# A streaming encoder step on one core: the last feed-forward down projection done with plain products, and the first pair of down weights begun one up tile sooner

## The chip, the cores and the metric

The kernel runs on one core of a Trainium2 chip. The time is that of one execution on the device, in microseconds (us); the kernel before was timed three times, at 1915.1, 1917.89 and 1915.02 us, with a median of 1915.1 us. One more execution was profiled.

## The reference, cut to what matters

The reference is one step of a two-layer encoder in float32, with a model width of 1024 and 544 tokens (512 of a prompt and 32 of a running stream). Layer 0 mixes tokens with a state-space block, layer 1 with retention; each layer then has a cross-attention to a memory and a convolutional feed-forward block (FFN), and one normalisation ends the step. The change concerns the FFN:

```python
def conv_ffn(h, conv_state, w_up, conv_w, conv_b, w_down):
    u = h @ w_up                       # 1024 -> 2 x 2816
    a, g = jnp.split(u, 2, axis=-1)
    ext = jnp.concatenate([conv_state, a], axis=1)
    conv = cw[0] * ext[:, 0:l] + cw[1] * ext[:, 1:l + 1] + cw[2] * ext[:, 2:l + 2] + conv_b
    y = (jax.nn.gelu(conv) * g) @ w_down   # 2816 -> 1024
# every layer:  x = x + conv_ffn(rms_norm(x, norm_ffn[i]), ...)
```

## The kernel before: tiles, stages and order

All activations are kept transposed, 128 features on the partitions by 544 tokens. So x is eight tiles `x[0..7]` of 128x544, and the 2816 hidden features are 22 tiles. Tokens are worked in two halves of 272 (`TH`), since a product of one half fills one bank of the accumulator.

Each float32 product is made of three passes of a reduced type: an operand is split into a high part (`hi`, a cast on ScalarE, L228) and a low part (`lo = value - hi`, on VectorE, L229), and hi.hi, hi.lo and lo.hi are added up on TensorE (PE). A plain projection (`dense`, with `dense_k`, L269) takes for each tile of 128 outputs 6 matmuls of 128x272 per tile of 128 inputs (two halves by three passes): 48 with the eight tiles of x. `dense2` does the first two outputs of a projection together, all but the last `late` input tiles first (by default one), so that they can begin before the last input tile is ready.

The FFN goes through its 22 hidden tiles in groups of 8, 8 and 6 (`FGROUPS`). For each tile it makes the two up products ("an up tile": 96 matmuls), the convolution, the gelu and the product with the gate (`gr`). After each group, `down` adds this group's share of the down projection to x. It does so by a Strassen-Winograd scheme with seven products in place of eight: the group's tiles are paired (`kps` pairs: 4, 4, 3), the eight output tiles are paired (p = 0..3), and each pair takes seven products, `step(p, 1)` to `step(p, 7)`, each of 3 x kps matmuls on one half (L1240). So a group of eight takes 4 x 7 x 12 = 336 matmuls, where a plain projection would take 384, and the group of six takes 252, where a plain one would take 288. Each product is added to x from the accumulator by VectorE (`add`, L1244, 128x272). Products that share an accumulator tile wait for each other's add.

The seven products need sums of weights. `unit` makes them for half an output pair's weights (a unit has at most two of the kps pairs, and pairs 0..3 have two units each): a load of the raw blocks on SyncE's queue (L1153, buffer `wr`), the sums `ws` on VectorE and GpSimd (L1163 to L1165; one buffer), the high part `hb` of the three plain blocks a11, a22, a12 (ScalarE, L1166), `lb = -hb` (ScalarE, L1167), the high part `wh` of the sums (ScalarE, L1174), a DMA from GpSimd's queue that reads the three blocks from memory again and adds them into `lb` (L1177, accumulate), and the low part `wl` of the sums (VectorE, L1180). `tokens` makes the matching sums of the hidden tiles (L1200 to L1203).

`begin` loads and starts the first unit of pair 0, `more` its DMA and the second unit; `rest` does all else: calls of `step` in a fixed order, with `load`, `make` and `close` of the next pair's units between them. Both are called around the up products of the group's last tile. The buffers are shared with the plain projections: `wr`, `wh` and `wl` have three slots each (one extra `wh` and `wl` for each fourth unit), `hb` and `lb` four, the accumulator four tiles `ps`. A scheduler orders each engine's instructions from the program's order and its own estimates; each engine then runs its list strictly in order.

When a tile of x is final after the last group, `resid_done` prepares what comes next. In layer 0 this is retention: the split of x times a gain (ScalarE L327 `xh`, VectorE L328 `xl`), the square (L334) and its sum `acc` (GpSimd, L337); the sum over features is made on PE (L365, L376) inside retention's first `dense2`, which has `late=2`. In layer 1 it is the end of the kernel: square, sum, y = x times a gain (L341), transposes of y on PE (L439), the sums of squares on PE (L365), scaling (L444, L445) and the stores. `add_x` (L392) is the add of a plain projection, 128x544.

Of the kernel before, what the change touches and what calls it, by code (L numbers as in the profile page):

```python
# [9 lines left out]
F32 = mybir.dt.float32  # L10
# [7 lines left out]
P = 128  # L18
# [81 lines left out]
def w_pairs(w):  # L100

    a = w.reshape(w.shape[0] // P, P, KT // 2, 2, P)
    out, kp = [], 0
    for nk in unit_sizes(a.shape[0] // 2):
        for mi, ki in ((1, 0), (0, 0), (1, 1), (0, 1)):
            out += [a[2 * (kp + n) + ki, :, :, mi].transpose(1, 0, 2) for n in range(nk)]
        kp += nk
    return np.concatenate(out, axis=2)


def layout(inp):
# [53 lines left out]
    d["w_g"] = np.stack([w_tiles(f["ffn_w_up"][i][:, FF:]) for i in range(2)])  # L165
    o = 0
    for n, g in enumerate(FGROUPS):
        d[f"w_d{n}"] = np.stack([w_pairs(f["ffn_w_down"][i][o * P:(o + g) * P]) for i in range(2)])
        o += g
    d["conv"] = np.concatenate([cols(a) for i in range(2) for a in (f["ffn_conv_w"][i], f["ffn_conv_b"][i][None])], axis=1)  # L170
    d["cconv"] = f["cache_conv"][:, 0].reshape(2, 2, NF, P).transpose(3, 0, 2, 1).reshape(P, 2 * NF * 2)
# [21 lines left out]
class Kernel:  # L193
# [945 lines left out]
    def unit(self, src, nk, j):  # L1139


        V, A, PL = self.nc.vector, self.nc.scalar, self.nc.gpsimd
        n = nk * P
        d, t = {}, {}

        def buf(tag):
            if j % 4 == 1:
                return self.fp.tile([P, 1024], F32R, tag=tag + "x", bufs=1, name=self.name(tag))
            return self.main.tile([P, 1024], F32R, tag=tag, bufs=3, name=self.name(tag))

        def load():
            t["raw"] = self.main.tile([P, 1024], F32, tag="wr", bufs=3, name=self.name("wr"))
            self.nc.sync.dma_start(out=t["raw"][:, :4 * n], in_=src)  # L1153

        def sums():
            raw = t["raw"]
            t["hs"], t["ls"] = buf("wh"), buf("wl")
            t["hb"], t["lb"] = (self.fp.tile([P, 768], F32R, tag=g, bufs=4, name=self.name(g)) for g in ("hb", "lb"))
            sf = t["sf"] = self.fp.tile([P, 1024], F32, tag="ws", bufs=1, name=self.name("ws"))[:, :4 * n]

            def two(a):
                return a.rearrange("p (b n) -> p b n", b=2)
            V.tensor_tensor(out=two(sf[:, :2 * n]), in0=two(raw[:, n:3 * n]), in1=raw[:, :n].unsqueeze(1).to_broadcast([P, 2, n]), op=OP.subtract)  # L1163
            V.tensor_tensor(out=sf[:, 2 * n:3 * n], in0=sf[:, n:2 * n], in1=raw[:, n:2 * n], op=OP.add)
            PL.tensor_tensor(out=sf[:, 3 * n:], in0=raw[:, 3 * n:4 * n], in1=sf[:, 2 * n:3 * n], op=OP.subtract)  # L1165
            A.copy(t["hb"][:, :3 * n], raw[:, n:4 * n])  # L1166
            A.activation(out=t["lb"][:, :3 * n], in_=t["hb"][:, :3 * n].bitcast(F32), func=AF.Copy, scale=-1.0)  # L1167
            for q, name in enumerate(("a11", "a22", "a12")):
                d[name] = t["hb"][:, q * n:(q + 1) * n], t["lb"][:, q * n:(q + 1) * n]
            for q, name in enumerate(("s3", "s1", "s2", "s4")):  # L1170
                d[name] = t["hs"][:, q * n:(q + 1) * n], t["ls"][:, q * n:(q + 1) * n]

        def first():
            A.copy(t["hs"][:, :4 * n], t["sf"])  # L1174

        def close():
            self.nc.gpsimd.dma_start(out=t["lb"][:, :3 * n], in_=src[:, n:4 * n], accum_op=OP.add)  # L1177

        def second():
            V.tensor_tensor(out=t["ls"][:, :4 * n], in0=t["sf"], in1=t["hs"][:, :4 * n].bitcast(F32), op=OP.subtract)  # L1180

        return d, load, sums, first, close, second
# [22 lines left out]
        two(t[0], ("t1", "t2"))  # L1205
        return d

    def down(self, src, kps, done):

        sizes = unit_sizes(kps)  # L1210
        first = [sum(sizes[:n]) for n in range(len(sizes))]
# [60 lines left out]
        def rest(y):  # L1272
# [24 lines left out]
            for p in range(1, KT // 2):  # L1297
# [5 lines left out]
                if go:  # L1303
                    load(p + 1)
                step(p - 1, 3)
                done(2 * p - 2)
                done(2 * p - 1)
                step(p, 6)
                if go:
                    make(p + 1, 0)  # L1310
                if p > 1:
                    step(p, 2)
                step(p, 4)
                if go:
# [2 lines left out]
                step(p, 5)  # L1317
                if go:
                    close(p + 1, 1)
            step(KT // 2 - 1, 3)  # L1320
            done(KT - 2)
            done(KT - 1)

        return begin, more, rest

# [4 lines left out]
    def ffn_layer(self, l):  # L1330
# [14 lines left out]
        for n, size in enumerate(FGROUPS):  # L1345
            ys, half = [], []
            last = n == len(FGROUPS) - 1
            begin, more, rest = self.down(io[f"w_d{n}"][l], size // 2, (lambda m: self.resid_done(m, final=l == 1)) if last else (lambda m: None))
            for i in range(size):
                if i == size - 1:  # L1350
                    begin()
                pa, pg = first if f == 0 else [self.dense(io[n_][l, f], xs) for n_ in ("w_a", "w_g")]
                if i == size - 1:
                    more()
                paf = pa.rearrange("p a b -> p (a b)")
                ext = slot(W + 2)
# [14 lines left out]
                PL.tensor_tensor(out=gr[:, TP:], in0=gr[:, TP:], in1=cv[:, TP + 2:W], op=OP.mult)  # L1371
                V.tensor_tensor(out=gr[:, :TP], in0=gr[:, :TP], in1=cv[:, :TP], op=OP.mult)
                half.append(gr)
                if len(half) == 2:
                    ys.append(self.tokens(half))
                    half = []
                f += 1
            rest(ys)
        nc.sync.dma_start(out=io["nconv"][l], in_=nco.rearrange("p f s c -> p (f s c)"))


    def retention(self, rp):
# [13 lines left out]
        tail = load("tail", [P, 16], io["tail"])  # L1396
        tails = load("tails", [TS, H], io["tails"])
        inner = load("inner", [P, H, TS], io["inner"])
        first = self.dense2([io["w_r"][n] for n in range(2)], xs, late=2, hooks=self.resid_r())
        r = self.r  # L1400
        cos, sin = st([P, T], "cos"), st([P, T], "sin")
        for t, n in ((cos, "cos"), (sin, "sin")):
# [231 lines left out]
```

## Time and profile before

| | us |
|---|---|
| median of three runs | 1915.1 |
| profiled execution, its own time | 1914.82 |
| its span in the trace | 1913.0 |
| what lies around the span | 1.82 |

| engine | busy us | share of the span |
|---|---|---|
| PE (matmul) | 1811.5 | 95% |
| VectorE (DVE) | 1196.2 | 63% |
| ScalarE (ACT) | 715.0 | 37% |
| GpSimd (POOL) | 393.1 | 21% |

The profile names an instruction by its engine, its line and the tiles it writes and reads: "PE L1240 MATMUL ps<-r,lb" is a matmul of line 1240 into an accumulator tile, with weights from `lb`. Times in the trace count from the start of the span. In rows in order of time, the first two numbers are start and duration, and "[0.55 <-DMA lb<-in_w_d]" says that the engine stood idle for 0.55 us before it and that this DMA ended the wait. Rows of a stretch of time give the busy time of an engine, its instructions in brackets and PEclk, the share of full speed that TensorE's clock was granted. The down projections' products stand in the trace from 516.7 us, 661.6 us and 783.8 us (layer 0) and from 1579.4 us, 1726.0 us and 1847.9 us (layer 1).

### The profile page before, as it was taken

What the parts mean: (1) busy time and instruction counts of PE and PEld (TensorE: products, weight loads), DVE (VectorE), ACT (ScalarE), POOL (GpSimd) and SP (SyncE); (2) the same over time, 40 slices, a digit from 0 to 9 for tenths busy, and PEclk for the clock granted to TensorE, in tenths of its full rate; (3) what the DMA queues carried; (4) which work ended last, traced back from release to release, by engine and by line L of the source; (5) the groups of instructions that cost most, each with busy time, mean ns of one, the idle gap of its engine ahead of it and who ended that gap; (6) DMA issues with size and microseconds to landing.
All of it is one profiled execution on the core that took longest, in us unless ns stands there. A gap on an engine that the chain in (4) does not pass through costs nothing. (4 is left out here: it accounts for less than half of the span.)

```text
span 1913.0 us, 33026 instructions
## 1 busy us (share of the span) xinstructions
PE 1811.5 (95%) x13551; PEld 1711.3 (89%) x13551; DVE 1196.2 (63%) x2143; ACT 715.0 (37%) x1073; POOL 393.1 (21%) x512
## 2 busy tenths in 40 slices
PE   8778899999999999889999999999999998999996
PEld 7467799899999989889899898998899998998995
DVE  7998875447756756765555646447554666566663
ACT  3244554334434424433123222233444343343343
POOL 4655310022211212310000100001002122122122
PEclk9978999999999999989999999999999999999998
DMA  6647733122443444432222222223312244345242
GB/s 223 207 122 175 209 134 111 34 89 89 122 111 100 121 100 118 93 103 86 80 88 90 77 78 74 99 69 107 102 67 78 89 114 108 100 108 124 92 102 70
DMA packets 75191, 203.73 MB, mean 106 GB/s; under 512 B 9953, under 2 KB 20577, under 8 KB 75041
## 3 DMA queue, kind: packets, MB, share of 16 engines
q1 hardware_dynamic: 65536, 175.79, 28.2%
q0 software_dynamic: 9216, 25.69, 8.0%
q8 instruction: 106, 1.74, 0.4%
q14 instruction: 45, 0.36, 0.1%
q10 hardware_dynamic: 288, 0.15, 0.0%
HBM read 188.47 MB, written 10.77 MB: 104 GB/s over the span
## 5 line engine op out<-in xcount | busy, mean ns | idle before, releaser
L269 PE MATMUL ps<-xh,wh 128*128 128x272 f32 x2432 | 508.0, 290 | 7.7 <-DVE x L392 3.6
L269 PE MATMUL ps<-xh,wl 128*128 128x272 f32 x2432 | 504.6, 289 | 1.0 <-DVE wl L229 1.0
L269 PE MATMUL ps<-xl,wh 128*128 128x272 f32 x2432 | 503.5, 288 | 1.8 <-DVE xl L328 1.8
L269 PEld LDWEIGHTS ps<-xh,wh 128*128 128x128 f32 x2432 | 383.7, 189 | 13.7 <-ACT r L334 3.8
L228 ACT CAST wh<-wr 128x1024 fp32r<-128x1024 f32 x192 | 201.0, 1051 | 517.0 <-PE ps L269 398.5
L269 PEld LDWEIGHTS ps<-xh,wl 128*128 128x128 f32 x2432 | 382.0, 189 | 4.4 <-issue 2.3
L269 PEld LDWEIGHTS ps<-xl,wh 128*128 128x128 f32 x2432 | 382.8, 189 | 2.4 <-DVE xl L328 2.1
L229 DVE TENSOR_TENSOR wl<-wr,wh 128x1024 fp32r<-128x1024 f32 x192 | 241.5, 1261 | 87.5 <-ACT wh L228 83.1
L269 PE MATMUL ps<-r,wh 128*128 128x272 f32 x1280 | 214.4, 289 | 3.0 <-ACT r L976 1.6
L269 PEld LDWEIGHTS ps<-r,wh 128*128 128x128 f32 x1280 | 180.8, 188 | 6.4 <-ACT r L228 3.0
L1240 PE MATMUL ps<-r,wh 128*128 128x272 f32 x704 | 141.6, 298 | 15.2 <-DVE x L1244 10.0
L1244 DVE TENSOR_TENSOR x<-ps,x 128x272 f32<-128x272 f32 x168 | 73.2, 439 | 122.0 <-PE ps L1240 120.4
L269 PE MATMUL ps<-r,wl 128*128 128x272 f32 x640 | 132.3, 288 | 0.0
L1240 PEld LDWEIGHTS ps<-r,wh 128*128 128x128 f32 x704 | 112.8, 193 | 20.6 <-DVE x L1244 8.3
L337 POOL TENSOR_TENSOR acc<-acc,r 128x544 f32<-128x544 f32 x36 | 57.6, 1601 | 251.0 <-ACT r L334 249.6
L1240 PE MATMUL ps<-r,hb 128*128 128x272 f32 x528 | 106.3, 296 | 1.6 <-DVE x L1244 1.6
L1240 PE MATMUL ps<-r,wl 128*128 128x272 f32 x352 | 103.3, 296 | 1.4 <-DVE wl L1180 1.4
L269 PEld LDWEIGHTS ps<-r,wl 128*128 128x128 f32 x640 | 100.2, 188 | 0.0
L1240 PE MATMUL ps<-r,lb 128*128 128x272 f32 x264 | 77.1, 302 | 13.5 <-DMA lb<-in_w_d 13.5
L1240 PEld LDWEIGHTS ps<-r,hb 128*128 128x128 f32 x528 | 85.7, 195 | 3.2 <-DVE x L1244 3.2
L1174 ACT CAST wh<-ws 128x1024 fp32r<-128x1024 f32 (+1 forms) x48 | 46.8, 976 | 98.8 <-POOL ws L1165 81.4
L392 DVE TENSOR_TENSOR x<-ps,x 128x544 f32<-128x544 f32 x48 | 34.5, 723 | 77.2 <-PE ps L269 77.2
(370 smaller groups left out, 2838.5 us busy)
## 6 DMA issues: line engine op xcount, KB each, us to landing
wr<-in_w_r SPq DMA_DIRECT2D x48, 512.0 KB, 3.7
wr<-in_w_a SPq DMA_DIRECT2D x44, 512.0 KB, 3.8
wr<-in_w_g SPq DMA_DIRECT2D x44, 512.0 KB, 3.7
wr<-in_w_d SPq DMA_DIRECT2D x40, 512.0 KB, 4.1
lb<-in_w_d POOLq DMA_DIRECT2D x40, 384.0 KB, 6.2
wr<-in_w_k SPq DMA_DIRECT2D x16, 512.0 KB, 4.7
wr<-in_w_v SPq DMA_DIRECT2D x16, 512.0 KB, 4.3
wr<-in_w_q SPq DMA_DIRECT2D x16, 512.0 KB, 4.1
```

What stands on the lines that cost most here:

```text
L228: self.nc.scalar.copy(hi, src)
L229: (self.nc.gpsimd if pool else self.nc.vector).tensor_tensor(out=lo, in0=src, in1=hi.bitcast(F32), op=OP.subtract)
L269: mm(ps[:, h, :TH], lhsT=ws[wi], rhs=x[xi][:, h * TH:(h + 1) * TH], start=start and n == 0, stop=stop and n == 2)
L337: add.tensor_tensor(out=self.acc, in0=self.acc, in1=sq, op=OP.add)
L392: self.nc.vector.tensor_tensor(out=self.halves(x), in0=src, in1=self.halves(x), op=OP.add)
L1174: A.copy(t["hs"][:, :4 * n], t["sf"])
L1240: mm(out, lhsT=w[wi], rhs=y[yi], start=start and k == 0 and m == 0, stop=stop and k == kps - 1 and m == 2, skip_group_check=not start)
L1244: self.nc.vector.tensor_tensor(out=x, in0=banks[p][i], in1=x, op=OP.add)
```

## The change

It has five parts.

1. The group of six tiles is a plain projection: its weights are laid out as plain tiles, each hidden tile is split as it is (`parts`), `dense2` makes outputs 0 and 1 and `dense` outputs 2 to 7, 36 matmuls each, and each is followed by `add_x` and `resid_done`. The hooks `done` in `down` go.
2. In `unit`, the low part of block a11 is made by VectorE from the raw block (128x256 for a whole unit) and no longer by the negative copy and the DMA: the copy has 512 columns and not 768, the DMA 256 KB and not 384 KB.
3. In the groups of eight, `begin` and `more` stand around the up products of the last tile but one, and not of the last.
4. In the last output pair, `step(p, 2)` comes after `step(p, 5)`, and not ahead of `step(p, 4)`.
5. Retention's first `dense2` has `late=1`.

```diff
-        d[f"w_d{n}"] = np.stack([w_pairs(f["ffn_w_down"][i][o * P:(o + g) * P]) for i in range(2)])
+        d[f"w_d{n}"] = np.stack([(w_tiles if n == len(FGROUPS) - 1 else w_pairs)(f["ffn_w_down"][i][o * P:(o + g) * P]) for i in range(2)])
...
             A.copy(t["hb"][:, :3 * n], raw[:, n:4 * n])
-            A.activation(out=t["lb"][:, :3 * n], in_=t["hb"][:, :3 * n].bitcast(F32), func=AF.Copy, scale=-1.0)
+            A.activation(out=t["lb"][:, n:3 * n], in_=t["hb"][:, n:3 * n].bitcast(F32), func=AF.Copy, scale=-1.0)
+            V.tensor_tensor(out=t["lb"][:, :n], in0=raw[:, n:2 * n], in1=t["hb"][:, :n].bitcast(F32), op=OP.subtract)
...
-            self.nc.gpsimd.dma_start(out=t["lb"][:, :3 * n], in_=src[:, n:4 * n], accum_op=OP.add)
+            self.nc.gpsimd.dma_start(out=t["lb"][:, n:3 * n], in_=src[:, 2 * n:4 * n], accum_op=OP.add)
...
                 step(p - 1, 3)
-                done(2 * p - 2)
-                done(2 * p - 1)
                 step(p, 6)
                 if go:
                     make(p + 1, 0)
-                if p > 1:
+                if p > 1 and go:
                     step(p, 2)
                 step(p, 4)
...
                 if go:
                     close(p + 1, 1)
+                else:
+                    step(p, 2)
             step(KT // 2 - 1, 3)
-            done(KT - 2)
-            done(KT - 1)
...
-            begin, more, rest = self.down(io[f"w_d{n}"][l], size // 2, (lambda m: self.resid_done(m, final=l == 1)) if last else (lambda m: None))
+            if not last:
+                begin, more, rest = self.down(io[f"w_d{n}"][l], size // 2)
             for i in range(size):
-                if i == size - 1:
+                if i == size - 2 and not last:
                     begin()
                 pa, pg = first if f == 0 else [self.dense(io[n_][l, f], xs) for n_ in ("w_a", "w_g")]
-                if i == size - 1:
+                if i == size - 2 and not last:
                     more()
...
-                if len(half) == 2:
+                if last:
+                    ys.append(self.parts(gr))
+                elif len(half) == 2:
                     ys.append(self.tokens(half))
                     half = []
                 f += 1
-            rest(ys)
+            if not last:
+                rest(ys)
+                continue
+            ahead = self.dense2([io[f"w_d{n}"][l, m] for m in range(2)], ys)
+            for m in range(KT):
+                ps = ahead[m] if m < 2 else self.dense(io[f"w_d{n}"][l, m], ys)
+                self.add_x(m, ps[:, :, :TH])
+                self.resid_done(m, final=l == 1)
...
-        first = self.dense2([io["w_r"][n] for n in range(2)], xs, late=2, hooks=self.resid_r())
+        first = self.dense2([io["w_r"][n] for n in range(2)], xs, hooks=self.resid_r())
```

How this moves instructions is seen at three places. The first is SyncE's queue of loads near the end of layer 0's first group; `in_w_a` and `in_w_g` are the up weights, and the last two pairs of them are those of tiles 6 and 7 of the group. Before:

```order
L233 DMA wr_5158<-in_w_a 128x1024
L233 DMA wr_5213<-in_w_g 128x1024
L1153 DMA wr_5284<-in_w_d 128x1024
L1153 DMA wr_5286<-in_w_d 128x1024
L233 DMA wr_5300<-in_w_a 128x1024
L233 DMA wr_5355<-in_w_g 128x1024
L1153 DMA wr_5462<-in_w_d 128x1024
L1153 DMA wr_5464<-in_w_d 128x1024
```

And with the change:

```order
L1153 DMA wr_5157<-in_w_d 128x1024
L1153 DMA wr_5159<-in_w_d 128x1024
L233 DMA wr_5174<-in_w_a 128x1024
L233 DMA wr_5229<-in_w_g 128x1024
L233 DMA wr_5315<-in_w_a 128x1024
L233 DMA wr_5370<-in_w_g 128x1024
L1153 DMA wr_5464<-in_w_d 128x1024
L1153 DMA wr_5466<-in_w_d 128x1024
```

The two raw units of pair 0 have moved ahead of the up weights of tile 6; those of pair 1 stay behind the up weights of tile 7.

The second place is ScalarE at the same point. `hb` is the high part of a raw unit (it waits for that unit's load), `lb` the negative copy, and `wh` from `wr` the high part of an up weight. Before:

```order
L228 CAST wh_5160<-wr_5158 128x1024
L1166 CAST hb_5290<-wr_5284 128x768
L1167 ACTIVATE lb_5291<-hb_5290 128x768
L228 CAST r_5136<-f_5001 128x272
L228 CAST wh_5215<-wr_5213 128x1024
L1366 ACTIVATE f_5127<-f_5119,conv 128x546
L1166 CAST hb_5413<-wr_5286 128x768
L1167 ACTIVATE lb_5414<-hb_5413 128x768
```

And with the change:

```order
L1166 CAST hb_5163<-wr_5157 128x768
L228 CAST wh_5012<-wr_5010 128x1024
L1167 ACTIVATE lb_5164<-hb_5163 128x512
L228 CAST r_4864<-f_4853 128x544
L1166 CAST hb_5287<-wr_5159 128x768
L228 CAST r_4874<-f_4869 128x544
L1167 ACTIVATE lb_5288<-hb_5287 128x512
L228 CAST wh_5067<-wr_5065 128x1024
```

The two casts of raw units stand one up tile sooner, ahead of the casts of the up weights of tile 5 (`wr_5010`, `wr_5065`), and the negative copies are a third shorter.

The third place is PE at the end of layer 1, where `ps_19729` is the accumulator of the last product and `ps_19624` that of the last plain output. Before:

```order
L1240 MATMUL ps_19729<-r_19395,wh_19706 128x272
L1240 MATMUL ps_19729<-r_19396,wh_19706 128x272
L1240 MATMUL ps_19729<-r_19395,wl_19707 128x272
L439 MATMUL ps_19833<-ident,r_19824 128x128
L439 MATMUL ps_19841<-ident,r_19824 128x128
L439 MATMUL ps_19849<-ident,r_19824 128x128
L365 MATMUL ps_19832<-ones,acc_15485 128x1
```

And with the change:

```order
L269 MATMUL ps_19624<-r_19279,wh_19627 128x272 x2
L269 MATMUL ps_19624<-r_19280,wh_19627 128x272 x2
L269 MATMUL ps_19624<-r_19279,wl_19628 128x272 x2
L439 MATMUL ps_19675<-ident,r_19371 128x128
L439 MATMUL ps_19675<-ident,r_19377 128x128
L439 MATMUL ps_19675<-ident,r_19426 128x128
L439 MATMUL ps_19675<-ident,r_19475 128x128
```

Before, three transposes (of x's tile 6) stand between the last product and the sums of squares (L365), and those of the tiles before it lie among the products; with the change, all 21 transposes of tiles 0 to 6 (the first four are shown) lie between the last plain matmul and the sums of squares.

More of the change, by code (lines that the diff above doesn't have):

```diff
@@ L1206, in tokens, with down @@
         return d
-    def down(self, src, kps, done):
+    def down(self, src, kps):
         sizes = unit_sizes(kps)
```

## The prediction

> **What bounds the kernel now.** I read the page first: which engine is full.
>
> ```profile
> span 1913.0 us, 33026 instructions
> PE 1811.5 (95%) x13551; PEld 1711.3 (89%) x13551; DVE 1196.2 (63%) x2143; ACT 715.0 (37%) x1073; POOL 393.1 (21%) x512
> PEclk9978999999999999989999999999999999999998
> L1240 PE MATMUL ps<-r,lb 128*128 128x272 f32 x264 | 77.1, 302 | 13.5 <-DMA lb<-in_w_d 13.5
> ```
>
> PE is the bound, and its clock is mostly granted in full. So time goes only where PE waits, where its clock is halved, or where it has fewer matmuls. Next the stretches of the work: a plain stretch (431.0), the plain ending of layer 0's attention up to the same kind of work (378.0), the four groups of eight, layer 0's group of six with retention's beginning (two rows), and layer 1's group of six with the tail.
>
> ```profile
> 378.00:431.00 53.00, 52.09 (x411) 51.52 (x411) 25.88 (x39) 18.62 (x25) 10.48 (x7) 1.00 0.25 80
> 431.00:516.70 85.70, 85.70 (x686) 85.66 (x686) 59.31 (x99) 41.71 (x53) 23.18 (x43) 1.00 0.38 107
> 516.70:574.60 57.90, 53.65 (x411) 51.70 (x410) 33.88 (x62) 19.14 (x23) 10.91 (x18) 1.00 0.44 107
> 661.60:720.90 59.30, 55.09 (x412) 53.30 (x411) 33.92 (x62) 19.20 (x23) 10.88 (x18) 0.97 0.43 105
> 783.80:849.70 65.90, 53.94 (x353) 50.35 (x351) 44.00 (x78) 24.40 (x37) 15.98 (x17) 0.87 0.38 104
> 849.70:887.30 37.60, 37.60 (x301) 37.59 (x301) 22.63 (x27) 9.46 (x12) 7.34 (x4) 1.00 0.26 85
> 1579.40:1639.10 59.70, 54.72 (x412) 53.21 (x411) 34.05 (x62) 19.21 (x23) 10.98 (x18) 0.97 0.43 104
> 1726.00:1785.00 59.00, 54.94 (x412) 53.28 (x411) 34.10 (x62) 19.19 (x23) 11.03 (x18) 0.97 0.43 105
> 1847.90:1896.70 48.80, 39.17 (x273) 35.72 (x271) 25.15 (x53) 20.23 (x33) 14.77 (x17) 0.97 0.22 47
> 1896.70:1913.00 16.30, 8.82 (x42) 7.30 (x42) 5.34 (x17) 4.21 (x7) 0.77 (x1) 0.53 0.38 137
> ```
>
> A plain stretch paces at 85.70 / 686 = 0.125 us a matmul. Each group of eight has some 411 matmuls (336 products and the next up tile's first), 51.4 us at that pace, and takes 57.9 to 59.7: 6.5, 7.8, 8.2 and 7.5 us lost, 30.0 in all. The group of six with retention's start has 252 + 384 matmuls and 15 small ones, and takes 103.5 us where the matmuls ask for 79.5.
>
> Last, single waits in order of time, in the first group and at the second group's start, and then the products of line 1240 alone in three short stretches, one in each of the other groups.
>
> ```profile
> 525.36 0.49 PE L1240 MATMUL ps<-r,wh 128*128 128x272 f32 x2 [0.96 <-DVE x L1244]
> 526.58 0.77 PE L1240 MATMUL ps<-r,wh 128*128 128x272 f32 x4 [0.61 <-ACT wh L1174]
> 538.31 0.39 PE L1240 MATMUL ps<-r,lb 128*128 128x272 f32 x1 [0.55 <-DMA lb<-in_w_d]
> 540.46 0.40 PE L1240 MATMUL ps<-r,lb 128*128 128x272 f32 x1 [0.37 <-DMA lb<-in_w_d]
> 549.06 0.39 PE L1240 MATMUL ps<-r,lb 128*128 128x272 f32 x1 [0.80 <-DMA lb<-in_w_d]
> 552.80 0.52 PE L1240 MATMUL ps<-r,hb 128*128 128x272 f32 x2 [0.21 <-DVE x L1244]
> 555.10 0.52 PE L1240 MATMUL ps<-r,wh 128*128 128x272 f32 x2 [0.53 <-DVE x L1244]
> ...
> 670.26 0.50 PE L1240 MATMUL ps<-r,wh 128*128 128x272 f32 x2 [0.97 <-DVE x L1244]
> 671.48 0.78 PE L1240 MATMUL ps<-r,wh 128*128 128x272 f32 x4 [0.60 <-ACT wh L1174]
> ```
>
> ```profile
> 672.00:675.40 3.40, 3.40 (x17) 3.40 (x17) 0.52 0.35 122
> 1590.00:1593.40 3.40, 3.40 (x19) 3.40 (x18) 0.55 0.31 101
> 1737.00:1740.40 3.40, 3.40 (x18) 3.40 (x17) 0.52 0.20 75
> ```
>
> Three kinds of loss stand here: weights of the first pair that are late (525.36, 526.58), the accumulating DMA into `lb` (538 to 549), and products that wait for the add of the product before them on the same accumulator tile (552.80, 555.10). In three of the four groups the two early waits are followed by 3.4 us at half clock (17 matmuls in place of 27), which costs 3.4 x 0.48 = 1.6 us.
>
> **The change part by part.** *Layer 0's group of six.* It gains 36 matmuls, +4.5 us. What goes are the product scheme's waits, the gap into retention and the half clock (0.87 over 65.9 us):
>
> ```profile
> 836.10 0.82 PE L269 MATMUL ps<-xh,wh 128*128 128x272 f32 x2 [2.27 <-ACT xh L327]
> 838.71 0.82 PE L269 MATMUL ps<-xl,wh 128*128 128x272 f32 x2 [1.79 <-DVE xl L328]
> 849.01 0.77 PE L376 MATMUL ps<-ident,rc 128*128 128x128 f32 x5
> 424.00 1.10 PE L365 MATMUL ps<-ones,acc 128*128 128x1 f32 x10
> L327 ACT ACTIVATE xh<-x,gains 128x544 fp32r<-128x544 f32 x40 | 29.8, 747 | 25.5 <-DVE x L1008 13.9 <-DVE x L392 11.6
> L328 DVE SCALAR_TENSOR_TENSOR xl<-x,gains,xh 128x544 fp32r<-128x544 f32 x40 | 42.5, 1072 | 4.1 <-ACT xh L327 4.1
> ```
>
> After: 288 + 384 = 672 matmuls by 0.125 = 84.0, the sums of squares (1.0, an estimate from 424.00, whose 1.10 overlaps what follows) and the broadcast (0.7, by 849.01) 1.7. The attention ending shows how much such an ending waits: 396 x 0.125 + 1.7 = 51.2 in 53.0, so 1.8. Together 87.5 against 103.5: **-16.0**. Bounds of the wait: 1.0 to 3.0, since the new ending has 36 matmuls a tile (4.5 us) where the old has 48. VectorE, busy 25.88 of 53.00 us in the 378.0 row, would be busy some 65% at that pace. With `late=1` the first output of retention's `dense2` runs through x's tiles 0 to 6, 42 matmuls or 5.25 us, before anything asks for tile 7, the one just finished; add (0.72, L392 below), cast (0.75) and low part (1.07) make 2.5 and fit in that, so I cost it at nothing; without that cover it is the 2.27 of 836.10.
>
> *Layer 1's group of six and the tail.*
>
> ```profile
> 1894.47 0.29 PE L1240 MATMUL ps<-r,wl 128*128 128x272 f32 x1
> 1896.68 0.55 PE L439 MATMUL ps<-ident,r 128*128 128x128 f32 x3 [1.92 <-ACT r L341]
> 1897.52 0.59 PE L365 MATMUL ps<-ones,acc 128*128 128x1 f32 x2 [0.30 <-POOL acc L337]
> 1901.33 0.90 PE L439 MATMUL ps<-ident,r 128*128 128x128 f32 x3
> L392 DVE TENSOR_TENSOR x<-ps,x 128x544 f32<-128x544 f32 x48 | 34.5, 723 | 77.2 <-PE ps L269 77.2
> ```
>
> Before, 49.6 us from 1847.9 to the sums of squares at 1897.52. After: 288 x 0.125 = 36.0, a wait of 1.8 as above, then 21 transposes, at about 0.1 us each (an estimate: 0.18 at the half clock of 1896.68), 2.1, beside which the last tile's add (0.72) and square run; 2.4 in all: 40.2, **-9.4**. The 20 sums of squares take 1897.52 to 1901.33, 3.8 us at a clock of 0.53; the row at 424.00 shows ten in 1.0 at full clock, so 2.1. Since the transposes close the gap ahead of them, I take the clock to hold: **-1.7**, bound 0. The rest of the tail stays. Together -11.1 (9.4 - 1.2 = 8.2 to 11.9).
>
> *The groups of eight.* (a) Weights of pair 0 come an up tile sooner. On ScalarE the late one shows:
>
> ```profile
> 512.43 0.83 ACT L1166 CAST hb<-wr 128x768 fp32r<-128x768 f32 x1 [5.05 <-DMA wr<-in_w_d]
> ```
>
> The load of the second unit held ScalarE, and with it the sums' casts, until 13 us ahead of 525.36. The start is one up tile sooner, 96 matmuls or 12 us, of which I count half, since `wr`'s slots come free only as up weights are cast; with 6 us more, most of the 1.6 us of 525.36 and 526.58 goes: -1.0 a group (0 to -1.6). (b) With it goes the half clock in three groups: -1.2 a group on average (0 or -1.6 each). (c) Block a11 no longer waits for the DMA; a12 still does, with a smaller one: the three DMA waits (1.7) fall to about 0.4: -1.3 (0 to -1.7). VectorE pays a 256-column subtract a unit, ScalarE a shorter copy; at 34 of 58 us busy, VectorE hides it. (d) Against it, in the last pair products 6, 4 and 3 now stand back to back on one accumulator tile with no other product between, each waiting for the add ahead: by 555.10 0.5 to 0.7 each, so +1.0 a group net of 552.80 and 555.10 (0 to +2). The sum is -2.5, in four groups **-10.0**. Bounds: all losses but the tails gone (2.5 left of 7.5), -20; none gone, 0.
>
> Here a rule speaks against (b). The clock rows say that 0.97 + 0.60 us of waits inside one 3.4 us stretch are followed by half clock. The Trainium skill ("TensorE: Matmul & The Clock Gate", section "Why this matters for your kernels") says to leave no idle gap over about 3 us between bursts; by that page no wait of these groups halves the clock, and the halving would stay: the sum would be 4.8 us smaller. The trace disagrees so far: the longest wait ahead of 672.0 is 0.97 us. I go by the trace.
>
> Sum against the profiled execution (span 1913.0 and 1.8 around it, 1914.8; the median of the runs is 1915.1): 1914.8 - 16.0 - 11.1 - 10.0 = 1877.7, so **1878 us**.
>
> **The rivals.** *The groups of eight give nothing.* The tails' add waits and a late `wh` eat what the DMA and the early start give. For: 552.80 and 555.10 show such waits, and the new order has more of them. Against: 525 to 549 hold over half the loss and both causes are touched. 1914.8 - 27.1 = 1888.
>
> *The half clock stays* (three groups): windows come for another reason than the early waits, and (b) gives nothing, 1877.7 + 4.8 = 1882.5. For: the first group has the same waits and a clock of 1.00. Against: in the other three the window follows the waits within 1 us. This is the result by the page's rule of the paragraph above.
>
> *The plain endings wait more.* A tile now comes every 4.5 us; if weights or `acc` (L337) pace it, 3 us each and the half clock of the tail stay: 1877.7 + 2.4 + 1.7 = 1882; in the worst case, with the first rival, 1892.
>
> *Slower: the up tiles starve.* The raw units of pair 0 now take `wr` slots ahead of two up tiles, and on ScalarE `hb`'s cast waits for them with the casts of tile 5's weights queued behind. If that wait is as at 512.43 (5.05) and the up weights' cast follows after `hb` (0.83) and takes 1.05, PE starves 6.9 us at each of four starts, and as long a wait is followed by half clock (1.6): +34.2, 1914.8 - 27.1 + 34.2 = 1922. It decides from 27.1 / 4 = 6.8 us a start. Against: an up tile is 96 matmuls, 12 us of cover, and weights stand a tile ahead in the other two slots.
>
> *The change doesn't do what it says* (the scheduler's order undoes the early start): the order shows both moves, so this falls under the first rival.
>
> **How the numbers follow.** Forecast 0.50 (1868 to 1887), nothing in the groups 0.20, half clock stays 0.14, plain endings wait 0.11, slower 0.05. The range reaches from all bounds at their best, 1914.8 - 16.8 - 11.9 - 20 = 1866, to the groups at nothing with waiting endings, 1892; it leaves out starvation and mixes beyond. A measurement of this kernel can tell about 0.2% (4 us) from no change. Every case but starvation is faster by more than that; small starvation lands within it. Faster 0.94, same 0.02, slower 0.04.
>
> **What would show it.** Right: 1847.9's stretch moved and about 40 us to the sums of squares; retention's first matmuls without the 2 us gaps; PEclk at 1.00 in the second, third and fourth group; `lb` waits at most one a pair. Wrong: rows "PE L269 <-ACT wh L228" of over 1 us ahead of the products (starvation); a group of eight at 59 us with more "<-DVE x L1244" (first rival); half clock in a group whose early waits are gone (second).

## The result and the profile after

The changed kernel takes 1891.0 us (median of four runs, 1890.25 to 1891.88), against 1916.3 us for the kernel before in the same measurement (four runs, 1915.02 to 1917.89): a ratio of 0.9868, with a 95% interval of 0.9851 to 0.9885. That is 25 us less, where 37 were forecast. The profiled execution took 1891.47 us, with a span of 1889.0 us: 24.0 less than before.

The page of the changed kernel, the rows that answer to those of before:

```profile
PE 1805.9 (96%) x13623; PEld 1709.6 (91%) x13623; DVE 1166.2 (62%) x2067; ACT 681.8 (36%) x1029; POOL 376.9 (20%) x480
PEclk9978999999999999999999999999999999999998
L1241 PE MATMUL ps<-r,wh 128*128 128x272 f32 x512 | 104.5, 299 | 12.8 <-DVE x L1245 12.8
```

Lines of the changed kernel are one higher from L1168 on: products are L1241, their adds L1245. The halved clock of layer 0's group of six is gone. The waits for the accumulating DMA (13.5 us before, in a row that has left the page) have made room for waits for adds: 12.8 us in this row, which had 10.0 before, though more than a quarter of the products is no longer there (1344 are left of 1848).

Now the same stretches of work. First the plain endings, of layer 0 (the down products; then retention's beginning) and of layer 1 (the down products; transposes and sums of squares; the rest):

```profile
788.70:824.80 36.10, 36.10 (x290) 36.10 (x289) 19.79 (x25) 16.41 (x23) 10.40 (x7) 1.00 0.40 126
824.80:874.80 50.00, 50.00 (x401) 49.76 (x400) 28.14 (x44) 12.67 (x16) 6.46 (x5) 1.00 0.26 89
1836.90:1873.00 36.10, 36.10 (x290) 36.10 (x289) 12.43 (x16) 14.46 (x21) 8.99 (x7) 1.00 0.11 34
1873.00:1877.30 4.30, 4.30 (x43) 4.29 (x42) 0.72 (x1) 1.30 (x2) 0.00 (x0) 1.00 0.00 0
1877.30:1889.00 11.70, 4.32 (x23) 2.91 (x21) 5.34 (x17) 3.10 (x5) 0.00 (x0) 0.53 0.53 191
```

TensorE is busy in every microsecond of the first four rows, at full clock. Layer 0's stretch is 36.1 + 50.0 = 86.1 us, where it was 103.5: -17.4. Layer 1's takes 36.1 and then, in order of time:

```profile
1873.09 2.45 PE L439 MATMUL ps<-ident,r 128*128 128x128 f32 x21
1875.38 0.28 PE L365 MATMUL ps<-ones,acc 128*128 128x1 f32 x2
...
1877.37 0.87 PE L439 MATMUL ps<-ident,r 128*128 128x128 f32 x4
```

From the first down product to the sums of squares it is 1875.4 - 1836.9 = 38.5 us (49.6 before, -11.1), and the sums of squares take 2.0 (3.8 before, -1.8), since the transposes leave no gap and the clock holds. Together the endings give 30.3 us.

Then the four groups of eight, with 409 or 410 matmuls in each stretch:

```profile
517.80:577.60 59.80, 55.14 (x409) 53.04 (x408) 33.98 (x64) 16.68 (x21) 9.65 (x16) 0.97 0.32 90
665.30:725.30 60.00, 55.03 (x410) 52.96 (x409) 34.63 (x65) 16.67 (x21) 9.66 (x16) 0.97 0.32 88
1567.30:1625.50 58.20, 53.45 (x409) 51.48 (x408) 34.01 (x64) 16.70 (x21) 9.61 (x16) 1.00 0.34 93
1713.20:1773.40 60.20, 54.97 (x409) 53.03 (x409) 34.13 (x64) 16.68 (x21) 9.66 (x16) 0.97 0.32 89
```

At 0.125 us a matmul they lose 8.7, 8.8, 7.1 and 9.1 us: 33.7 where it was 30.0. The groups give nothing; they take 3.7 us. Endings and groups make -26.6; the span is 24.0 shorter, and the 2.6 between lie outside of these stretches (not split further). The waits in the first group are these:

```profile
527.38 0.48 PE L1241 MATMUL ps<-r,wh 128*128 128x272 f32 x2 [1.40 <-DVE x L1245]
528.62 0.52 PE L1241 MATMUL ps<-r,wh 128*128 128x272 f32 x2 [0.63 <-DVE x L1245]
544.38 0.39 PE L1241 MATMUL ps<-r,lb 128*128 128x272 f32 x1 [0.36 <-DMA lb<-in_w_d]
552.03 0.52 PE L1241 MATMUL ps<-r,wh 128*128 128x272 f32 x2 [0.54 <-DVE x L1245]
554.34 0.52 PE L1241 MATMUL ps<-r,hb 128*128 128x272 f32 x2 [0.53 <-DVE x L1245]
```

One DMA wait is left of three, as forecast. But the first wait has grown from 0.96 to 1.40 us, the wait for `wh` behind it has become one for an add, and three of the four groups still have half clock after it (0.97 in the rows above). What stands in front of the first wait on VectorE and ScalarE:

```profile
525.82 1.07 DVE L229 TENSOR_TENSOR r<-f,r 128x544 fp32r<-128x544 f32 x1 [0.38 <-ACT r L228]
526.81 0.43 DVE L1245 TENSOR_TENSOR x<-ps,x 128x272 f32<-128x272 f32 x1
```

```profile
514.95 1.05 ACT L1175 CAST wh<-ws 128x1024 fp32r<-128x1024 f32 x1 [1.31 <-POOL ws L1165]
515.90 0.85 ACT L1366 ACTIVATE f<-f,conv 128x546 f32<-128x546 f32 x1
```

The add that releases TensorE stands behind the low part of a token sum (L229 at 525.82), the last link of the last hidden tile's own chain: convolution (L1366), gelu, gate, token sums, split. In ScalarE's queue that convolution stands directly behind a cast of the second pair's weights, which waits for GpSimd; in the kernel before it stood behind a cast of the first pair's (513.17, with the convolution at 514.11). On VectorE, the second pair's last low part (521.59, 1.23 us) and the third pair's first sums (524.07 and 525.02, 1.1 us) stand between the product with the gate (520.69) and that split. Which of these the wait comes from is a question for the experiments.

### The profile page after: what moved, and what is told of

Read it like the earlier page. It is cut to its first block, busy times and chain, and to the rows that moved or that the text cites. A ratio compares the mean times of both kernels' runs of the same rounds, so it can differ in the third digit from the quotient of the medians.

```text
span 1889.0 us, 32940 instructions
## 1 busy us (share of the span) xinstructions
PE 1805.9 (96%) x13623; PEld 1709.6 (91%) x13623; DVE 1166.2 (62%) x2067; ACT 681.8 (36%) x1029; POOL 376.9 (20%) x480
## 5 line engine op out<-in xcount | busy, mean ns | idle before, releaser
L228 ACT CAST wh<-wr 128x1024 fp32r<-128x1024 f32 (+1 forms) x208 | 213.9, 1034 | 575.8 <-PE ps L269 472.9
L229 DVE TENSOR_TENSOR wl<-wr,wh 128x1024 fp32r<-128x1024 f32 (+1 forms) x208 | 256.3, 1235 | 92.2 <-ACT wh L228 87.5
L269 PE MATMUL ps<-r,wh 128*128 128x272 f32 x1664 | 278.4, 289 | 3.0 <-ACT r L976 1.6
L269 PEld LDWEIGHTS ps<-r,wh 128*128 128x128 f32 x1664 | 235.1, 188 | 6.4 <-ACT r L228 3.0
L269 PE MATMUL ps<-r,wl 128*128 128x272 f32 x832 | 172.0, 288 | 0.0
L269 PEld LDWEIGHTS ps<-r,wl 128*128 128x128 f32 x832 | 130.3, 188 | 0.0
L1241 PE MATMUL ps<-r,wh 128*128 128x272 f32 x512 | 104.5, 299 | 12.8 <-DVE x L1245 12.8
L1241 PEld LDWEIGHTS ps<-r,wh 128*128 128x128 f32 x512 | 83.5, 196 | 16.3 <-DVE x L1245 9.4
L1245 DVE TENSOR_TENSOR x<-ps,x 128x272 f32<-128x272 f32 x112 | 47.6, 436 | 78.3 <-PE ps L1241 78.2
L1241 PE MATMUL ps<-r,hb 128*128 128x272 f32 x384 | 75.3, 289 | 2.1 <-DVE x L1245 2.1
L1241 PE MATMUL ps<-r,wl 128*128 128x272 f32 x256 | 76.1, 297 | 0.3
L1363 POOL COPY nco<-f 128x2 f32<-128x2 f32 x44 | 31.4, 713 | 224.6 <-DVE f L1361 224.6
L1368 DVE SCALAR_TENSOR_TENSOR f<-f,conv,f 128x546 f32<-128x546 f32 x88 | 68.9, 783 | 1.4
```

Of the source, the lines that this page charges most:

```text
L228: self.nc.scalar.copy(hi, src)
L229: (self.nc.gpsimd if pool else self.nc.vector).tensor_tensor(out=lo, in0=src, in1=hi.bitcast(F32), op=OP.subtract)
L269: mm(ps[:, h, :TH], lhsT=ws[wi], rhs=x[xi][:, h * TH:(h + 1) * TH], start=start and n == 0, stop=stop and n == 2)
L1241: mm(out, lhsT=w[wi], rhs=y[yi], start=start and k == 0 and m == 0, stop=stop and k == kps - 1 and m == 2, skip_group_check=not start)
L1245: self.nc.vector.tensor_tensor(out=x, in0=banks[p][i], in1=x, op=OP.add)
L1363: PL.tensor_copy(out=nco[:, f, 0], in_=ext[:, TP:TP + 2])
```

## The experiments

The theory after the traces: the endings give all of the gain, and the groups lose because what parts 2 and 3 remove there is replaced by the last hidden tile's chain and by a new order of products. Rivals: the prediction's reason (late weights of the first pair), and the added VectorE work by itself. Times are medians, each with its ratio to the kernel before in the same measurement. There were four measurements: the changed kernel; e1 to e4; e5 to e7; e8 and e9. The kernel before took 1916.3, 1914.7, 1914.4 and 1914.2 us in them, so between measurements the ratios tell more than the microseconds.

| kernel | us | ratio (95%) |
|---|---|---|
| changed kernel | 1891.0 | 0.9868 (0.9851 to 0.9885) |
| e1: parts 1 and 5 | 1884.5 | 0.9844 (0.9826 to 0.9861) |
| e2: and part 2 | 1891.1 | 0.9876 (0.9858 to 0.9893) |
| e3: and part 3 | 1886.4 | 0.9858 (0.9839 to 0.9878) |
| e4: and part 4 | 1884.7 | 0.9849 (0.9827 to 0.9870) |
| e5: e2 with ordering edges | 1886.2 | 0.9856 (0.9835 to 0.9877) |
| e6: e3, second pair's weights shared | 1875.4 | 0.9798 (0.9773 to 0.9824) |
| e7: changed kernel, late=2 | 1889.1 | 0.9868 (0.9849 to 0.9887) |
| e8: e5, part 2 in pairs 3 and 4 only | 1882.0 | 0.9829 (0.9808 to 0.9849) |
| e9: changed, part 2 in pairs 3 and 4 only, one edge | 1885.6 | 0.9856 (0.9836 to 0.9876) |

**e1: the endings alone.** The changed kernel with parts 2 to 4 undone:

```diff
-                if i == size - 2 and not last:
+                if i == size - 1 and not last:
...
-            V.tensor_tensor(out=t["lb"][:, :n], in0=raw[:, n:2 * n], in1=t["hb"][:, :n].bitcast(F32), op=OP.subtract)
...
-                if p > 1 and go:
+                if p > 1:
```

> Only the group of six as a plain projection, with the shorter wait in retention's first products (parts 1 and 5); the groups of eight stay as before. From the two traces the two plain endings gave 16.9 and 12.5 us and the groups of eight took 4.3 us back. If the groups' loss comes from parts 2 to 4, this kernel is faster than the changed one: 1916 - 29 = 1887 us (1884 to 1889). The rival, that the plain endings themselves disturb the groups of eight (other buffers' slots, other layout), has it at the changed kernel's time, 1891.

1884.5 us, 2.5 below the expected value and within its range: the endings alone give 30 us, and all runs (1882.15 to 1886.32) lie below all of the changed kernel's. So parts 2 to 4 cost some 5 us together (6.5 by the medians, 4.6 by the ratios, whose intervals overlap), and the plain endings do not disturb the groups.

**e2: part 2**, on top of e1:

```diff
-            A.activation(out=t["lb"][:, :3 * n], in_=t["hb"][:, :3 * n].bitcast(F32), func=AF.Copy, scale=-1.0)
+            A.activation(out=t["lb"][:, n:3 * n], in_=t["hb"][:, n:3 * n].bitcast(F32), func=AF.Copy, scale=-1.0)
+            V.tensor_tensor(out=t["lb"][:, :n], in0=raw[:, n:2 * n], in1=t["hb"][:, :n].bitcast(F32), op=OP.subtract)
...
-            self.nc.gpsimd.dma_start(out=t["lb"][:, :3 * n], in_=src[:, n:4 * n], accum_op=OP.add)
+            self.nc.gpsimd.dma_start(out=t["lb"][:, n:3 * n], in_=src[:, 2 * n:4 * n], accum_op=OP.add)
```

> Parts 1 and 5 with part 2: block a11's low part on VectorE. In the changed kernel's trace the waits for the accumulating DMA fell from 2.3 to 0.7 us a group. If that is part 2's doing alone: 1887 - 4 x 1.5 = 1881 us. The rival, that the extra subtract on VectorE lengthens the chain ahead of the adds as much, has it at 1887.

Neither: 1891.1, 6.6 us slower than e1. The waits for the DMA did not shrink, they grew (first group, 2.06 us in one of them). The two traces show where, on ScalarE and GpSimd. (e1's is of its fastest run, 1882.15 us, and e2's of its slowest, 1893.88, so sums over the two traces overstate the difference; the places do not depend on that.) In e1, whose first group begins at 514.7, the fourth pair's casts and DMAs:

```profile
534.99 1.59 ACT L1166 CAST hb<-wr 128x768 fp32r<-128x768 f32 x2 [0.40 <-PE ps L1240]
...
537.62 0.86 POOL L1177 DMA_DIRECT2D lb<-in_w_d  x1 [5.12 <-DVE ws L1164]
```

And in e2, whose first group begins at 516.7:

```profile
541.07 1.59 ACT L1166 CAST hb<-wr 128x768 fp32r<-128x768 f32 x2 [2.46 <-PE ps L1241]
...
543.48 0.86 POOL L1178 DMA_DIRECT2D lb<-in_w_d  x1 [8.41 <-DVE x L1245]
...
551.97 0.39 PE L1241 MATMUL ps<-r,lb 128*128 128x272 f32 x1 [2.06 <-DMA lb<-in_w_d]
```

The cast comes 20.3 us after the group's beginning in e1 and 24.4 in e2; both wait for TensorE to be done with a buffer of `hb`. In e2's order of instructions TensorE does the third pair's product 1 and two thirds of its product 2 ahead of the second pair's product 4, the last that reads its `hb` and `lb`; in e1 only the first two matmuls of each stand ahead of it. The program's text is the same there, so the scheduler moved the products forward. That it did so because it no longer expects a DMA ahead of block a11 is likely, but not shown.

**e5: the order put back.** e2 with edges on TensorE that restore e1's order of those products:

```diff
+                    if (p, i) in ((1, 4), (1, 3)) and (k, m) == (kps - 1, 2):
+                        banks["end", i] = ins
+                    if p > 1 and i in (1, 7) and (k, m) == (0, 2):
+                        self.tc.add_manual_dep(ins.ins, banks["end", 4 if p == 2 else 3].ins.name, ...)
```

> The kernel of parts 1, 2 and 5 (1891.1 us) with four ordering edges on TensorE: products 1 and 7 of the third output pair may go on past their second matmul only after product 4 of the second pair, and those of the fourth pair only after product 3 of the second. That is the order that the kernel of parts 1 and 5 (1884.5 us) has by itself. Theory: part 2 loses because the scheduler, no longer expecting a DMA for block a11, puts the third pair's products ahead of the second pair's last ones, which hold the buffers of hb and lb, so that the next weights start late. Then the waits for the accumulating DMA fall from 3.7 to below 2 us a group and the time to 1880 to 1885 us. Rival: the subtract itself is what VectorE can't bear; then it stays at 1891.

1886.2, just outside of the expectation: 4.9 of the 6.6 us come back by the medians of the two measurements, 3.8 by the ratios, whose intervals overlap. In the first group the wait for the DMA is 0.21 us, and over the four groups these waits make 4.5 us where e2 has 13.2 and e1 7.6. So the order was most of part 2's loss. What is left stands in the first wait, 1.88 us in place of e1's 0.96 (1.82, 1.02 and 1.84 in the other groups):

```profile
527.96 0.49 PE L1241 MATMUL ps<-r,wh 128*128 128x272 f32 x2 [1.88 <-DVE x L1249]
```

So the rival may have a share too: the second pair's two subtracts (0.42 us each) stand on VectorE ahead of the last tile's token sums. e8 tests this.

**e8: part 2 where VectorE has time.** e5, but the first two pairs keep copy and DMA for all three blocks:

```diff
+        at = n if j > 3 else 0
...
+            A.activation(out=t["lb"][:, at:3 * n], in_=t["hb"][:, at:3 * n].bitcast(F32), func=AF.Copy, scale=-1.0)
+            if at:
+                V.tensor_tensor(out=t["lb"][:, :n], in0=raw[:, n:2 * n], in1=t["hb"][:, :n].bitcast(F32), op=OP.subtract)
...
+            self.nc.gpsimd.dma_start(out=t["lb"][:, at:3 * n], in_=src[:, n + at:4 * n], accum_op=OP.add)
```

> The kernel of parts 1, 2 and 5 with the ordering edges (1886.2 us), with part 2 only in the third and fourth output pair; the first two pairs keep the negative copy and the DMA for all three blocks. Theory: what part 2 still costs there is the second pair's two subtracts (0.42 us each) in VectorE's queue ahead of the last hidden tile's token sums: the first wait of a group falls from 2.0 to 1.1 us, the DMA waits stay at 0.7 to 2.3, and the time is 1880 to 1883. If the first wait has another cause, it stays at 1886.

1882.0, within the expectation, and the first wait is back at e1's length (0.99, 0.75 and 0.99 in the other groups), with the wait for `wh` of 0.60 us behind it:

```profile
527.47 0.49 PE L1243 MATMUL ps<-r,wh 128*128 128x272 f32 x2 [0.96 <-DVE x L1251]
```

Its four groups take 231.2 us (e1 234.4, e2 244.3, e5 235.9). It is the fastest of the kernels that leave nothing out: 9 us below the changed kernel by the medians and 7.5 by the ratios, with an interval that lies just below that one's (0.9849 against 0.9851). Against e1 (2.5 us) the intervals overlap.

**e3: the sooner start**, on top of e1 (at both calls):

```diff
-                if i == size - 1 and not last:
+                if i == size - 2 and not last:
```

> Parts 1 and 5 with part 3: the first pair's weights begun one up tile sooner. The prediction's reason (those weights are what the first waits of a group wait for, and the half clock follows them) has it at 1887 - 4 x 2.2 = 1878 us. The theory after the traces, that these waits are for the last hidden tile's own chain (convolution, gelu, token sums) and that the sooner start puts the second pair's casts and sums in front of it, has it no faster than 1887, and up to 4 us slower.

1886.4, 1.9 slower than e1, with overlapping intervals: no gain, and no loss that can be told. The prediction's 1878 is out. The trace shows half of its reason right. The first group:

```profile
521.23 0.39 PE L1240 MATMUL ps<-r,lb 128*128 128x272 f32 x1 [0.66 <-DMA lb<-in_w_d]
525.72 0.49 PE L1240 MATMUL ps<-r,wh 128*128 128x272 f32 x2 [0.36 <-DVE x L1244]
527.02 0.52 PE L1240 MATMUL ps<-r,wh 128*128 128x272 f32 x2 [0.30 <-DVE x L1244]
539.01 0.39 PE L1240 MATMUL ps<-r,lb 128*128 128x272 f32 x1 [0.72 <-DMA lb<-in_w_d]
542.51 0.39 PE L1240 MATMUL ps<-r,lb 128*128 128x272 f32 x1 [0.83 <-DMA lb<-in_w_d]
546.45 0.39 PE L1240 MATMUL ps<-r,lb 128*128 128x272 f32 x1 [1.05 <-DMA lb<-in_w_d]
```

The wait for `wh` (0.6) is gone, with a wait for an add of 0.3 in its place, the first wait is 0.36, 1.30, 0.54 and 1.32 us in the four groups (0.95 to 1.07 in e1), and all four run at a clock of 1.00. But four DMA waits make 3.3 us where e1 has two with 1.7: the accumulating DMAs of the third and fourth pair are issued within 5 us of each other (from 533.59 to 538.26; in e1 from 530.72 to 538.85), and land after 7.8 us in the median, where e1's take 6.0.

**e6: the second pair's weights taken away.** e3, where the second output pair of each group uses the first pair's weights. All matmuls and adds stay; the second pair's loads, sums, casts, low parts and DMAs are left out.

```diff
+                if p == 1:
+                    units[p, n] = (units[0, n][0],) + ((lambda: None),) * 5
+                    continue
```

> The kernel of parts 1, 3 and 5 (1886.4 us), where in each group of eight the second output pair uses the first pair's weights, so that its loads, sums, casts, low parts and accumulating DMAs are left out; all matmuls and adds stay. Theory: the first wait of a group (<-DVE x, 0.5 to 1.5 us in that kernel) is the last hidden tile's chain of convolution, gelu and token sums, held up on VectorE and ScalarE by the second pair's weights; it then falls to 0.3 us or less in each group. The prediction's reason, late weights of the first pair, has it unchanged, since those are made as before. The time by the theory: 4 x 1 to 2 us less, 1878 to 1883; by the other, about 1886.

1875.4, 11 us below e3, more than the theory had. In the first group no wait stands before 542.7:

```profile
542.71 0.39 PE L1243 MATMUL ps<-r,lb 128*128 128x272 f32 x1 [0.18 <-DMA lb<-in_w_d]
545.80 0.39 PE L1243 MATMUL ps<-r,lb 128*128 128x272 f32 x1 [1.07 <-DMA lb<-in_w_d]
```

The first waits are gone in all four groups, although the first pair's weights are made as in e3. So they are not late weights of the first pair; they come from the next pairs' work on the engines that the last hidden tile's chain needs. Which engine, the traces tell. On ScalarE nothing is gained: the third pair's casts have moved into the place of the second's, and the last convolution begins 2.3 us ahead of the group's first product in both kernels (513.72 against 516.0 in e3, 515.01 against 517.3 in e6). On VectorE e3 has a low part and two sums (at 521.77 and 522.72, 1.1 us) between the last product with the gate and the last splits:

```profile
519.28 1.23 DVE L1180 TENSOR_TENSOR wl<-ws,wh 128x1024 fp32r<-128x1024 f32 x1 [0.16 <-ACT wh L1174]
```

In e6 these 2.3 us are not there, the splits follow the token sums directly, and VectorE waits for TensorE:

```profile
521.59 2.16 DVE L229 TENSOR_TENSOR r<-f,r 128x544 fp32r<-128x544 f32 x3
524.65 2.23 DVE L1247 TENSOR_TENSOR x<-ps,x 128x272 f32<-128x272 f32 x5 [0.90 <-PE ps L1243]
```

Not all of the 11 us are the first waits. Over the four groups the first two waits made 4.8 us in e3; the waits for the DMA fell from 10.6 to 3.6 as well, and a wait for a late `wl` (3.0 in all) is new.

**e4 and e7: parts 4 and 5.** e4 is e1 with part 4:

```diff
-                if p > 1:
+                if p > 1 and go:
                     step(p, 2)
...
+                else:
+                    step(p, 2)
```

> Parts 1 and 5 with part 4: in the last pair product 2 after product 5. In the changed kernel's trace three products in a group's last part wait 0.7 us each for the add ahead (before: 0.4 and 0.7), and the next up tile's weights came 0.6 and 0.3 us late twice more. If part 4 does this, 1887 + 4 x 2 = 1895 us; if not (the scheduler's order follows from part 2 or 3), 1887.

1884.7 against 1884.5. Compared engine by engine, e4's instructions stand in the very order of e1's, and the changed kernel's in that of the same kernel without part 4: the scheduler undoes the move in the text. The back-to-back products in a group's last part come from parts 2 and 3 together: the changed kernel has three waits of 0.53 us for an add there, part 3 alone (e3) two and part 2 alone (e2) one. As e1 and e4 are one program, their profiles show what one program does from run to run. The first and fourth group of e1, then of e4:

```profile
514.70:572.50 57.80, 53.52 (x411) 51.71 (x410) 33.91 (x62) 19.08 (x23) 10.94 (x18) 1.00 0.44 108
1706.80:1764.60 57.80, 53.43 (x411) 51.63 (x409) 34.08 (x62) 19.05 (x23) 11.14 (x18) 1.00 0.45 107
```

```profile
520.80:580.30 59.50, 55.21 (x410) 53.17 (x409) 34.11 (x62) 19.03 (x23) 11.13 (x18) 0.97 0.42 105
1714.00:1772.40 58.40, 53.77 (x410) 51.65 (x410) 34.11 (x62) 19.06 (x23) 11.14 (x18) 1.00 0.45 106
```

e7 is the changed kernel with retention's wait as before:

```diff
-        first = self.dense2([io["w_r"][n] for n in range(2)], xs, hooks=self.resid_r())
+        first = self.dense2([io["w_r"][n] for n in range(2)], xs, late=2, hooks=self.resid_r())
```

> The changed kernel with late=2 in retention's first products again (part 5 undone). By the prediction's cover (42 matmuls, 5.25 us, against 2.5 us for add, cast and low part) part 5 costs and gives nothing: 1891. If with late=1 the wait for x's last tile were what limits, late=2 would be slower or faster by up to 2.3 us.

1889.1 with the same ratio as the changed kernel, 0.9868: part 5 costs and gives nothing that can be told.

**e9: the sooner start without the subtracts.** The changed kernel with part 2 in the last two pairs only (as in e8), part 4 taken back, and one edge at a group's end:

```diff
+                    if (p, i, k, m) == (3, 7, kps - 1, 2):
+                        banks["seven"] = ins
+                    if (p, i, k, m) == (2, 3, 0, 0):
+                        self.tc.add_manual_dep(ins.ins, banks["seven"].ins.name, ...)
```

> The changed kernel (1891.0 us) with part 2 only in the third and fourth output pair, part 4 taken back (it moves no instruction), and one ordering edge on TensorE: product 3 of the third pair after product 7 of the fourth, which takes apart the back-to-back products at a group's end. Theory: the first wait falls by the 0.84 us of the second pair's subtracts (1.6 to 0.8), one of three add waits (0.7) at the end goes and the next up weights come in time, the DMA waits stay below 1 us: 4 x 2 to 3 us less, 1879 to 1883, and faster than the kernel of parts 1 and 5 alone (1884.5). If the sooner start is what hurts, it stays above 1886.

1885.6, outside of the expectation, though 5 us better than the changed kernel by the medians (2.3 by the ratios, whose intervals overlap). The first wait fell to 0.57 us in the first group and to 1.13, 0.59 and 1.31 in the others (1.40, 1.87, 1.33 and 1.47 in the changed kernel), and the clock is 1.00 in all four groups. The edge took away one wait for an add at the group's end, but in its place there is a new wait for the sums of the fourth pair (`wh` and `wl`, 0.5 + 0.7 us). TensorE's waits in the first group, with their total, number and longest:

```profile
PE ps L1243 <- DVE x L1251: 1.9, 4, 0.6
PE ps L1243 <- DMA lb<-in_w_d: 0.9, 3, 0.4
PE ps L1243 <- DVE wl L1183: 0.7, 1, 0.7
PE ps L1243 <- ACT wh L1177: 0.5, 1, 0.5
```

Whether the sooner start can pay with still another order stays open.

## Why the prediction was right in its direction and too large

- **Layer 0's ending: right.** Forecast -16.0, measured -17.4. The endings wait less than the 1.8 us taken from the attention's ending: nothing at all.
- **Layer 1's ending: right.** Forecast -11.1, measured -12.9, with the sums of squares at full clock (-1.7 forecast, -1.8 measured).
- **Groups of eight, step (a): this is the step that failed.** "With 6 us more, most of the 1.6 us of 525.36 and 526.58 goes." I had read the cast of 512.43, and the `wh` that 526.58 waits for, as the first pair's. In the kernel before ScalarE has

```profile
481.62 0.82 ACT L1166 CAST hb<-wr 128x768 fp32r<-128x768 f32 x1
488.92 0.83 ACT L1166 CAST hb<-wr 128x768 fp32r<-128x768 f32 x1 [0.21 <-DMA wr<-in_w_d]
...
504.53 0.83 ACT L1166 CAST hb<-wr 128x768 fp32r<-128x768 f32 x1 [1.32 <-DMA wr<-in_w_d]
...
525.48 1.05 ACT L1174 CAST wh<-ws 128x1024 fp32r<-128x1024 f32 x1 [2.23 <-POOL ws L1165]
```

  The first two, with an up weight's cast and a convolution between them, are `hb_5290` and `hb_5413` in the order of instructions shown ahead of the prediction: the first pair's two units, 36 us and more ahead of 525.36. So 504.53 and 512.43 are the second pair's. The first pair's last `wh` is cast at 513.17, 12 us ahead, and the `wh` that 526.58 waits for is the second pair's last. The first pair was not late, and a sooner start of it could not take away waits for it. It took away another: with the first pair's work done earlier the second pair's last `wh` comes sooner (at 518.21 in e3, 2.2 us after the group's first product, where it came 8.8 us after), and the 0.6 us are gone. The larger wait is for the last hidden tile's chain, which weights' work on VectorE lengthens: e6 removes it without touching the first pair, e5 lengthens it with two subtracts. Forecast -1.0 a group; measured +0.5 in the changed kernel's first group (0.96 + 0.61 us before, 1.40 + 0.63 after). The growth goes with part 2's subtracts: without those of the first two pairs (e9) the first wait is 0.6 to 1.3 us.
- **Step (b), the half clock: forecast -1.2 a group, measured none** in the changed kernel (three of four groups at 0.97, as before), since the first waits stayed. In e3, e6 and e9, where they add up to 0 to 1.6 us, none of the twelve groups has it. Their sum alone does not tell these groups from the others: two groups each of e3 and e9 wait 1.4 to 1.6 us in all, and in e1 groups with 0.96 + 0.60 and 0.95 + 0.60 are halved. They differ in the second wait, 0.3 us or none against 0.6. What starts the half clock is not shown. The rival by the page of the Trainium skill ("TensorE: Matmul & The Clock Gate", "Why this matters for your kernels"), that gaps under some 3 us don't halve the clock and the halving would stay, comes near in its number for this step and not in its reason: here no single wait ahead of the halving is longer than 1.9 us in the changed kernel, and in e3 and e9, whose waits are a little shorter, it is gone.
- **Step (c), the DMA: right for the changed kernel** (1.7 to 0.4 in the first group), but not for the reason given. Part 2 alone makes these waits worse (e2); only with the order that part 3, or the edges of e5, gives does the shorter DMA show. I had priced the instruction and not what the scheduler does with it.
- **Step (d), the group's end: right in size, wrong in place.** Forecast +1.0 a group; the waits for adds there grew from 0.7 to 1.6 us, and the next up tile's low parts are late by 0.6 us where it was 0.2. But these adds are not in the last pair. They are in the third, whose products 6 and 4 now stand directly behind 7 and 6 on one accumulator tile (552.03 and 554.34), and product 3 behind 5 (558.96); before, 4 stood behind 6 with half a product between (552.80) and 5 behind 4 (555.10). The last pair's products lie among the next up tile's matmuls and wait for no add, before or after. Nor is the cause part 4, which moves no instruction.
- **Together**, without the half clock, steps (a), (c) and (d) changed the waits of the first group by +0.5 - 1.3 + 1.3 = +0.5 us, where -1.3 was forecast.
- **The first rival** ("the groups of eight give nothing", 1888) was what happened, with 3 us more on the endings and 6 us lost in the groups and beside them. It had 0.20. The range held since it reached to that case. That the endings gave more than forecast is luck for the total: without it the result would have been some 1894 us.

## What to carry to other kernels

A wait that names an engine is ended by the last link of a chain: before moving what seems to hold it, follow that engine's queue back and see whose work fills it (by counting the casts from a place that is known, since a name such as `hb` stands for every pair's), and what will take the place when it goes. With a scheduler between text and engines, an edit changes the order of things that it doesn't touch: compare the order of instructions, engine by engine, with the price of the edit, and pin the order by an edge where it matters. Where a saving scheme with short waits (252 matmuls) ends on the critical path, the plain one with more work and no waits (288) can be faster by 13 to 17 us, the idle clock and the tail included.

## What the runs showed of the hardware

Half clock in the groups of eight is no fixed property of a program: e1 and e4 are the same instructions, and the first group has a clock of 1.00 in one profile and 0.97 in the other, with nearly the same two waits ahead of it (0.96 and 0.61 us, 1.02 and 0.61). Over the profiles of all eleven kernels, 21 of the 32 groups whose second wait was 0.6 us fell below 1.00, and none of the 12 whose second wait was 0.3 us or none; this goes together, and no run separates it as a cause. Accumulating DMAs of 384 KB landed after 7.8 us in the median where four of six were issued within 5 us (e3), and after 6.0 where those four were issued over 8 us (e1). Over the whole run the medians of 32 such DMAs are 7.2 and 6.6 us; that the closeness is the cause was not tested.

A product that directly follows another on the same accumulator tile, with VectorE's add of 128x272 between, starts 0.82 us after the last matmul of the first (551.21 to 552.03 and 558.14 to 558.96 in the changed kernel); without a wait it would be the pace of 0.125.
